# Opening stage: modulation on TensorE for three half parts of four, and another order of loads and stores

## The chip, the cores and the metric

The kernel runs on one core of a Trainium2 chip. The metric is the time of one execution in microseconds (us) on the device, of which the median of several runs is given. All data are float32 for 256 positions of width 1024.

## The reference

Two transformer blocks follow each other. The change touches the head of the first one alone:

```python
c_act = jax.nn.silu(c)
mod = c_act @ ada_w[l] + ada_b[l]
shift1, scale1, gate1, shift2, scale2, gate2 = [m[:, None, :] for m in jnp.split(mod, 6, axis=-1)]
h = rms_norm(x, norm1_g[l]) * (1 + scale1) + shift1
z = h @ w_in[l]
q, k, v, p, g_attn, g_pool = jnp.split(z, split_at, axis=-1)
```

`c` is one row of 1024 numbers and `ada_w` is 1024 x 6144, so `mod` is a product of one row with a matrix. Attention, pooling, the gates, a gated feed-forward block, and then a second block with a dense part and one with eight experts come behind. At the end of each of the second block's two layers stands `gate * (p[i] @ ple_proj_w[i])`; its product `p[i] @ ple_proj_w[i]` depends on inputs only, and the kernel computes it in the opening stage and parks it in memory.

## The kernel before, in words

Everything is held with features on the 128 partitions: `h` is a tile of 128 x 8 x 256 (feature in its group, group of features, position). A weight matrix is loaded in tiles of 128 x 4096 float32 (2 MB) named raw, of which there are three buffers used in turn (`load`, L138). To multiply nearly exactly at the speed of a narrow type, `split` (L158) makes of a piece of raw a high part (ScalarE copies it to a rounded type, L172, tile whi) and a low part (VectorE subtracts, L173, tile wlo), and `mm3` (L201) issues three products: high by high, high by low, low by high. Matmuls of other helpers go through `mm` (L199). A matmul of two plain float32 operands shows in the trace as two instructions.

The opening stage is written out by hand: within `tc.manual_schedule` (L623) VectorE, TensorE and ScalarE execute in the order in which the lines issue. SyncE issues the loads in the order in which they are written, and a load whose raw buffer is still read waits, with all that stand behind it on SyncE. The pieces are these:

- `Projected` (L557), once for each of two layers (e0 and e1): `parts` splits the two inputs, `sums(j)` makes 12 products of 256 columns for j from 0 to 3, so 48 in all, and `out(j)` copies the result from the accumulator; every second copy is stored to memory (tile kept, L586), issued by ScalarE.
- `rstd` (L265): the norm of `h`, summed over partitions by a matmul with a matrix of ones (L271), which is a part of the constants' tile ct, loaded at L366.
- `half_modulation` (L507), four times: part 1 is the scale and part 0 the shift, each in halves of 512 columns. A raw tile of `ada_w` is loaded in four pieces of 512 KB. `steps` lets VectorE multiply eight rows of 128 x 512 by `c` and add them up (L518, L520, into the tile sums); `total` sums that over the partitions with 8 matmuls by a column of ones; `put` adds `ada_b`.
- `scaled` (L533) and `shifted` (L538) put scale and shift of one half on `h` (tiles xn, and the pair xh and xl).
- `unit` (L544) splits a quarter of a half of `w_in`, and `products` (L548) multiplies it: 24 products of 256 columns, four units to each half, 96 a half. The first half of `w_in` comes in a raw tile, the second in a tile of its own (last_in).
- `distances` (L596) and `flipped` (L606): the bias of the attention, eight instructions of 512 columns on TensorE for four flips.

The order of TensorE before is: e0's sums, the norm's matmul and the distances among them; scale[0]'s sum ahead of e0's last sums; the e1 sums with shift[0]'s among them; the four products of the first half, with scale[1]'s sum after two of them; the four flips; shift[1]'s sum; the four products of the second half. In the code, `scale[0][0]`, `[1]` and `[2]` are steps, total and put:

```python
            scale[1][0](range(8))
            products(0, 1, us[1])
            scale[1][1]()
            products(0, 2, us[2])
            scale[1][2]()
            scaled(1)
            shift[1][0](range(8))
            products(0, 3, us[3])
```

Behind the manual order stand the norms of q and k, the value block of `w_in` (`gemm_v`), the attention, and the rest of the modulation: `modulation` (L384), stepped by VectorE along the following splits, which takes its loads of `ada_w` through the same raw buffers.

Of the kernel before, what the change touches and what calls it, by code (L numbers as in the profile page):

```python
# [10 lines left out]
F32 = mybir.dt.float32  # L11
# [4 lines left out]
OP = mybir.AluOpType  # L16
# [4 lines left out]
D = 1024  # L21
# [83 lines left out]
def kernel(ctx: ExitStack, tc: tile.TileContext, d, vat, cat, out, upto=99):  # L105
# [28 lines left out]

    raws = [wp, wp, wp]
    turn = [0]

    def load(src, pieces=1, columns=1, also=None):  # L138
# [6 lines left out]
        for i in range(0, a, a // pieces):  # L145
            for j in range(0, b, b // columns):
                ks, cs = slice(i, i + a // pieces), slice(j, j + b // columns)
                nc.sync.dma_start(v[:, ks, cs], src[:, ks, cs])
        if also is not None:
# [114 lines left out]

    def rstd(sq, n, both=False):  # L265

        o = bank("mm")[:, 0]
        if len(sq.parts) == 1:
            acc = sq.parts[0]
            dve.tensor_add(acc[:, 0], acc[:, 0], acc[:, 1])  # L270
            pe.matmul(o, cst("ones"), acc[:, 0], start=True, stop=True)  # L271
        else:
            for i in range(4):
                mm(o, cst("ones"), sq.parts[i // 2][:, i % 2], i == 0, i == 3)
        r = inv_sqrt(o, n, 256)
        return (r, o) if both else r
# [88 lines left out]
    nc.sync.dma_start(h, d["xT"])  # L365
    nc.sync.dma_start(ct, d["cst"])  # L366

# [127 lines left out]
    with stage("b1", po=1, acc=3, mm=4) as bp:  # L495
# [4 lines left out]
        xn = bp.tile([128, 8, 256], F32, name="xn", tag="ga")  # L500
        last_in = bp.tile([128, 4, 1024], F32, name="raw", tag="qkvp")


        sums = bp.tile([128, 4, 512], F32, name="sums", tag="gp")
        ps = [[bank("mm") for _ in range(2)] for _ in range(2)]

        def half_modulation(part, hf):  # L507

            at = part * 1024 + hf * 512
            o = part * 8 + hf * 4  # L510
            r = load(ada_w[:, :, at:at + 512], pieces=4)
            st = {}

            def steps(ks):
                for k in ks:
                    a, c = sums[:, 2 * (1 - part) + k % 2], sc[:, k:k + 1]
                    if k < 2:
                        dve.tensor_scalar(a, r[:, k], c, None, op0=OP.mult)  # L518
                    else:
                        dve.scalar_tensor_tensor(a, r[:, k], c, a, op0=OP.mult, op1=OP.add)  # L520

            def total():
                p = st["p"] = flat(bank("acc"))
                for i in range(2):
                    for j in range(4):
                        mm(p[:, j:j + 1], sums[:, 2 * (1 - part) + i, j * 128:j * 128 + 128],
                           cst("ones")[:, 0:1], i == 0 and j == 0, i == 1)

            def put():
                dve.tensor_add(mod[:, o:o + 4], st["p"][:, :4], vec[:, vat["ada_b"] + o:vat["ada_b"] + o + 4])  # L530
            return steps, total, put

# [24 lines left out]
        class Projected:  # L557
# [23 lines left out]
            def out(self):  # L581
# [3 lines left out]
                if j % 2:  # L585
                    nc.scalar.dma_start(kept[self.l][:, 2 * j - 2:2 * j + 2], t)  # L586

# [22 lines left out]

        scale, shift, ws = [], [], []
        scale.append(half_modulation(1, 0))
        second_projection = projection(1)
        shift.append(half_modulation(0, 0))
        ws.append(load(w_in[:, :4, :1024], pieces=2))
        scale.append(half_modulation(1, 1))
        shift.append(half_modulation(0, 1))
        for i in range(0, 4, 2):
            nc.sync.dma_start(last_in[:, i:i + 2], w_in[:, 4 + i:6 + i, :1024])
        ws.append(last_in)  # L620
        e0 = Projected(0, *first_projection, ("ath", "atl"))
        e1 = Projected(1, *second_projection, ("pqh", "pql"))
        with tc.manual_schedule(engines={dve.engine, pe.engine, act.engine}):  # L623
# [6 lines left out]
            e0.out()  # L630
            dve.tensor_copy(r1, rstd(sq, D))
            e0.out()
            e0.sums(2)
            distances()
            e0.out()
            scale[0][0](range(8))
            e0.sums(3)
            scale[0][1]()
            e0.out()
            e1.parts()  # L640
            scale[0][2]()
            scaled(0)
            e1.sums(0)
            e1.out()
            shift[0][0](range(8))
            e1.sums(1)
            e1.out()
            shift[0][1]()
            e1.sums(2)
            shift[0][2]()  # L650
            shifted(0)
            e1.out()
            e1.sums(3)
            us = [unit(0, 0)]
            e1.out()
            us += [unit(0, i) for i in range(1, 4)]
            products(0, 0, us[0])
            scale[1][0](range(8))
            products(0, 1, us[1])
            scale[1][1]()  # L660
            products(0, 2, us[2])
            scale[1][2]()
            scaled(1)
            shift[1][0](range(8))
            products(0, 3, us[3])
            for i in range(4):
                flipped(i)
            shift[1][1]()
            us = [unit(1, 0)]
            shift[1][2]()  # L670
            shifted(1)
            us += [unit(1, i) for i in range(1, 4)]
# [797 lines left out]
```

## Time and profile before

| | |
|---|---|
| median of 3 runs | 2002.33 us (2001.86 to 2008.63) |
| the profiled execution, its own time | 2010.97 us |
| its span, first to last instruction | 2009.2 us |
| mean granted TensorE clock in it | 0.984 |
| TensorE busy | 97% of the span |
| VectorE, ScalarE, GpSimd busy | 80%, 65%, 3% |
| read from memory | 531.19 MB |

A granted clock of 1.00 is the full clock and 0.50 half of it. Matmuls overlap in the pipeline, so the distance between two starts, not the duration of one, tells what a product costs; a merged line gives the time from the first start to the last end. An idle time is put down to what ended it. Times in the rows are counted from the span's start. The opening stage reaches to about 83 us.

### The profile page before, as it was taken

The numbers are of one execution on the slowest core, as the hardware profiler recorded it, in microseconds if no ns is written. First come the engines' busy times: TensorE is split into PE (matmuls) and PEld (weight loads), VectorE is DVE, ScalarE is ACT, GpSimd is POOL, SyncE is SP. The second block draws the span as 40 slices with busy tenths as digits, with TensorE's granted clock in tenths as the row PEclk, the third lists the DMA queues.
The fourth block names the chain that finished last, engine by engine and source line by source line (L and its number), as shares of the span: only waits on it lengthen the run. The fifth ranks groups of instructions, "written<-read, shape, count | busy, mean of one in ns | idle before, by whom it ended". The sixth has DMA issues, their size and how long they took to land. (4 is left out here: it accounts for less than half of the span.)

```text
span 2009.2 us, 29483 instructions
## 1 busy us (share of the span) xinstructions
PE 1950.1 (97%) x11943; PEld 1727.2 (86%) x11943; DVE 1598.9 (80%) x1898; ACT 1305.8 (65%) x1628; POOL 64.2 (3%) x64
## 2 busy tenths in 40 slices
PE   6999999999989999999999999999989999999998
PEld 5889899998989999989788888888868888888887
DVE  6667687777765555867799998889879888988988
ACT  4456465566554444665688787777767777777775
POOL 1002000000000000101200000000000000000000
PEclk8899999999999999999999999999999999999999
DMA  9566655463426454624599998999969999999990
GB/s 371 207 242 220 246 220 205 163 229 133 153 103 227 148 207 177 225 85 168 199 370 371 344 381 298 361 371 356 365 250 377 359 351 372 343 363 374 352 370 24
DMA packets 221681, 536.32 MB, mean 267 GB/s; under 512 B 4798, under 2 KB 8006, under 8 KB 221153
## 3 DMA queue, kind: packets, MB, share of 16 engines
q1 hardware_dynamic: 220560, 531.12, 72.4%
q8 instruction: 95, 1.56, 0.3%
q10 hardware_dynamic: 576, 2.10, 0.3%
q0 software_dynamic: 400, 1.15, 0.2%
q14 instruction: 50, 0.40, 0.1%
HBM read 531.19 MB, written 3.16 MB: 266 GB/s over the span
## 5 line engine op out<-in xcount | busy, mean ns | idle before, releaser
L173 DVE TENSOR_TENSOR wlo<-raw,whi 128x1024 fp32r<-128x1024 f32 (+1 forms) x949 | 1121.6, 1223 | 195.2 <-ACT whi L172 187.6
L172 ACT ACTIVATE whi<-raw 128x1024 fp32r<-128x1024 f32 (+1 forms) x957 | 983.0, 1055 | 380.6 <-PE pt L199 276.0
L199 PE MATMUL pt<-xh,whi 128*128 128x256 f32 x1536 | 444.5, 290 | 15.2 <-ACT xh L803 3.4
L199 PE MATMUL pt<-xl,whi 128*128 128x256 f32 x1536 | 442.5, 288 | 1.2 <-DVE xl L287 1.0
L199 PE MATMUL pt<-xh,wlo 128*128 128x256 f32 x1536 | 441.7, 288 | 1.8 <-DVE wlo L173 1.7
L199 PE MATMUL pt<-wlo,xh 128*128 128x512 f32 (+1 forms) x1000 | 381.4, 381 | 1.6 <-DVE wlo L173 1.6
L199 PE MATMUL pt<-whi,xl 128*128 128x512 f32 (+1 forms) x1000 | 381.9, 382 | 0.0
L199 PE MATMUL pt<-whi,xh 128*128 128x512 f32 (+1 forms) x1000 | 380.6, 381 | 0.2
L199 PEld LDWEIGHTS pt<-xh,whi 128*128 128x128 f32 x1536 | 299.8, 195 | 19.8 <-ACT xh L286 5.8
L199 PEld LDWEIGHTS pt<-xl,whi 128*128 128x128 f32 x1536 | 300.2, 195 | 5.2 <-issue 2.9
L199 PEld LDWEIGHTS pt<-xh,wlo 128*128 128x128 f32 x1536 | 300.3, 195 | 4.4 <-DVE wlo L173 2.4
L199 PEld LDWEIGHTS pt<-wlo,xh 128*128 128x128 f32 x1000 | 188.4, 188 | 40.7 <-DVE wlo L173 3.2
L199 PEld LDWEIGHTS pt<-whi,xh 128*128 128x128 f32 x1000 | 188.6, 189 | 36.2 <-ACT xh L1116 0.6
L199 PEld LDWEIGHTS pt<-whi,xl 128*128 128x128 f32 x1000 | 188.6, 189 | 34.8 <-issue 0.7
L199 PE MATMUL pt<-whi,gtl 128*128 128x512 f32 x448 | 178.9, 399 | 0.0
L199 PE MATMUL pt<-wlo,gth 128*128 128x512 f32 x448 | 177.3, 396 | 0.0
L199 PE MATMUL pt<-whi,gth 128*128 128x512 f32 x448 | 161.2, 403 | 0.0
L199 PE MATMUL fa<-gl,whi 128*128 128x256 f32 x400 | 112.6, 282 | 0.0
L199 PE MATMUL fa<-gh,whi 128*128 128x256 f32 x400 | 112.6, 281 | 0.0
L199 PE MATMUL fa<-gh,wlo 128*128 128x256 f32 x400 | 112.6, 281 | 0.0
L199 PEld LDWEIGHTS pt<-wlo,gth 128*128 128x128 f32 x448 | 84.2, 188 | 25.1 <-DVE wlo L173 4.6
L199 PEld LDWEIGHTS pt<-whi,gtl 128*128 128x128 f32 x448 | 84.3, 188 | 17.1
(296 smaller groups left out, 1995.9 us busy)
## 6 DMA issues: line engine op xcount, KB each, us to landing
raw<-in_moe_w_dram SPq DMA_DIRECT2D x168, 2048.0 KB, 9.1
raw<-in_dense_w_dram SPq DMA_DIRECT2D x21, 2048.0 KB, 7.9
raw<-in_w_in_dram SPq DMA_DIRECT2D x18, 2048.0 KB, 9.1
raw<-in_w_up_dram SPq DMA_DIRECT2D x10, 2048.0 KB, 10.1
raw<-in_ada_w_dram SPq DMA_DIRECT2D x16, 1024.0 KB, 7.8
raw<-in_w_down_dram SPq DMA_DIRECT2D x5, 2048.0 KB, 8.2
raw<-in_ada_w_dram SPq DMA_DIRECT2D x16, 512.0 KB, 11.4
raw<-in_w_o_dram SPq DMA_DIRECT2D x4, 2048.0 KB, 7.8
```

Of the source, the lines that this page charges most:

```text
L172: act.activation(hv, v, AF.Copy)
L173: eng.tensor_sub(lv, v, hv.bitcast(F32))
L199: pe.matmul(o, a, b, start=start, stop=stop, skip_group_check=True)
```

## The change

`half_modulation` becomes a class with the same parts. Three half parts are no longer stepped by VectorE: `total` multiplies the raw tile of `ada_w` (stationary) with the column of `c` (moving, one column) in 8 x 4 matmuls. The scale's second half is stepped by VectorE as before, from a tile of its own (fourth), and summed with a new tile of ones (ones1), which the norm's matmul takes as well and which GpSimd fills. The sums keep two tiles instead of four.

The loads come in another order: shift[0]'s half stands directly behind scale[0]'s, the second layer's projection behind them, the constants behind the scale's second half, and the second half of `w_in` now goes into a raw tile. The four stores of the projections are issued by SyncE, behind the last load of the opening, instead of ScalarE.

On TensorE, all of e0 comes first, with the distances ahead of the norm; then the long sums of scale[0] and shift[0] one behind the other; then e1; the four products of the first half without a break; the short sum of scale[1] and the long one of shift[1]; the flips; and the products of the second half.

```diff
--- before.py
+++ after.py
@@ -133,6 +133,7 @@
         return w.rearrange("(k p) n -> p k n", p=128)
 
     raws = [wp, wp, wp]
+    loaded = []
     turn = [0]
 
     def load(src, pieces=1, columns=1, also=None):
@@ -145,7 +146,7 @@
         for i in range(0, a, a // pieces):
             for j in range(0, b, b // columns):
                 ks, cs = slice(i, i + a // pieces), slice(j, j + b // columns)
-                nc.sync.dma_start(v[:, ks, cs], src[:, ks, cs])
+                loaded[:] = [nc.sync.dma_start(v[:, ks, cs], src[:, ks, cs]).ins]
         if also is not None:
             _, c, e = also.shape
             w = t[:, a * b:a * b + c * e].rearrange("p (a b) -> p a b", a=c)
@@ -262,13 +263,13 @@
         add.parts, add.n = st, 0
         return add
 
-    def rstd(sq, n, both=False):
+    def rstd(sq, n, both=False, ones=None):
 
         o = bank("mm")[:, 0]
         if len(sq.parts) == 1:
             acc = sq.parts[0]
             dve.tensor_add(acc[:, 0], acc[:, 0], acc[:, 1])
-            pe.matmul(o, cst("ones"), acc[:, 0], start=True, stop=True)
+            pe.matmul(o, cst("ones") if ones is None else ones, acc[:, 0], start=True, stop=True)
         else:
             for i in range(4):
                 mm(o, cst("ones"), sq.parts[i // 2][:, i % 2], i == 0, i == 3)
@@ -363,7 +364,6 @@
 
     first_projection = projection(0)
     nc.sync.dma_start(h, d["xT"])
-    nc.sync.dma_start(ct, d["cst"])
 
     sc = cp.tile([128, 8], F32, name="sc")
     c8 = vec[:, vat["c"]:vat["c"] + 8]
@@ -498,37 +498,44 @@
         w_in = rows(d["w_in"][0])
         x = pair([128, 8, 256], "x")
         xn = bp.tile([128, 8, 256], F32, name="xn", tag="ga")
-        last_in = bp.tile([128, 4, 1024], F32, name="raw", tag="qkvp")
-
-
-        sums = bp.tile([128, 4, 512], F32, name="sums", tag="gp")
+        fourth = bp.tile([128, 8, 512], F32, name="raw", tag="qkvp")
+        sums = bp.tile([128, 2, 512], F32, name="sums", tag="gp")
+        ones1 = bp.tile([128, 128], F32, name="ones1", tag="pdf")
+        nc.gpsimd.memset(ones1, 1.0)
+
+
         ps = [[bank("mm") for _ in range(2)] for _ in range(2)]
 
-        def half_modulation(part, hf):
-
-            at = part * 1024 + hf * 512
-            o = part * 8 + hf * 4
-            r = load(ada_w[:, :, at:at + 512], pieces=4)
-            st = {}
-
-            def steps(ks):
+        class HalfModulation:
+
+
+            def __init__(self, part, hf, r=None):
+                at = part * 1024 + hf * 512
+                self.o = part * 8 + hf * 4
+                src = ada_w[:, :, at:at + 512]
+                self.r = load(src, pieces=4) if r is None else r
+                if r is not None:
+                    for k in range(0, 8, 2):
+                        nc.sync.dma_start(r[:, k:k + 2], src[:, k:k + 2])
+
+            def steps(self, ks):
                 for k in ks:
-                    a, c = sums[:, 2 * (1 - part) + k % 2], sc[:, k:k + 1]
+                    a, c = sums[:, k % 2], sc[:, k:k + 1]
                     if k < 2:
-                        dve.tensor_scalar(a, r[:, k], c, None, op0=OP.mult)
+                        dve.tensor_scalar(a, self.r[:, k], c, None, op0=OP.mult)
                     else:
-                        dve.scalar_tensor_tensor(a, r[:, k], c, a, op0=OP.mult, op1=OP.add)
-
-            def total():
-                p = st["p"] = flat(bank("acc"))
-                for i in range(2):
+                        dve.scalar_tensor_tensor(a, self.r[:, k], c, a, op0=OP.mult, op1=OP.add)
+
+            def total(self, src=None, n=8):
+                self.p = flat(bank("acc"))
+                for k in range(n):
                     for j in range(4):
-                        mm(p[:, j:j + 1], sums[:, 2 * (1 - part) + i, j * 128:j * 128 + 128],
-                           cst("ones")[:, 0:1], i == 0 and j == 0, i == 1)
-
-            def put():
-                dve.tensor_add(mod[:, o:o + 4], st["p"][:, :4], vec[:, vat["ada_b"] + o:vat["ada_b"] + o + 4])
-            return steps, total, put
+                        mm(self.p[:, j:j + 1], (self.r if src is None else src)[:, k, j * 128:(j + 1) * 128],
+                           sc[:, k:k + 1] if src is None else ones1[:, 0:1], k == j == 0, k == n - 1)
+
+            def put(self):
+                o = self.o
+                dve.tensor_add(mod[:, o:o + 4], self.p[:, :4], vec[:, vat["ada_b"] + o:vat["ada_b"] + o + 4])
 
         def scaled(hf):
             gains("norm1_g", 0, 4 * hf, 4)
@@ -583,7 +590,8 @@
                 o = 2 * (j % 2)
                 act.activation(t[:, o:o + 2], p, AF.Copy)
                 if j % 2:
-                    nc.scalar.dma_start(kept[self.l][:, 2 * j - 2:2 * j + 2], t)
+                    with tc.issue_after(loaded[0]):
+                        nc.sync.dma_start(kept[self.l][:, 2 * j - 2:2 * j + 2], t)
 
         rb = bp.tile([BUCKETS + 1, H], F32, name="rb")
         oh = bp.tile([BUCKETS + 1, 384], F32, name="ohb", tag="wt", bufs=2)
@@ -609,15 +617,14 @@
             act.activation(bias[:, 2 * i:2 * i + 2], pf, AF.Copy)
 
         scale, shift, ws = [], [], []
-        scale.append(half_modulation(1, 0))
+        scale.append(HalfModulation(1, 0))
+        shift.append(HalfModulation(0, 0))
         second_projection = projection(1)
-        shift.append(half_modulation(0, 0))
         ws.append(load(w_in[:, :4, :1024], pieces=2))
-        scale.append(half_modulation(1, 1))
-        shift.append(half_modulation(0, 1))
-        for i in range(0, 4, 2):
-            nc.sync.dma_start(last_in[:, i:i + 2], w_in[:, 4 + i:6 + i, :1024])
-        ws.append(last_in)
+        scale.append(HalfModulation(1, 1, fourth))
+        nc.sync.dma_start(ct, d["cst"])
+        shift.append(HalfModulation(0, 1))
+        ws.append(load(w_in[:, 4:, :1024], pieces=2))
         e0 = Projected(0, *first_projection, ("ath", "atl"))
         e1 = Projected(1, *second_projection, ("pqh", "pql"))
         with tc.manual_schedule(engines={dve.engine, pe.engine, act.engine}):
@@ -628,47 +635,43 @@
                 sq(h[:, 2 * j:2 * j + 2])
             e0.sums(1)
             e0.out()
-            dve.tensor_copy(r1, rstd(sq, D))
-            e0.out()
-            e0.sums(2)
             distances()
             e0.out()
-            scale[0][0](range(8))
+            dve.tensor_copy(r1, rstd(sq, D, ones=ones1))
+            e0.sums(2)
+            e0.out()
             e0.sums(3)
-            scale[0][1]()
             e0.out()
+            scale[0].total()
+            scale[0].put()
+            scaled(0)
+            shift[0].total()
             e1.parts()
-            scale[0][2]()
-            scaled(0)
+            shift[0].put()
+            shifted(0)
             e1.sums(0)
             e1.out()
-            shift[0][0](range(8))
             e1.sums(1)
             e1.out()
-            shift[0][1]()
             e1.sums(2)
-            shift[0][2]()
-            shifted(0)
+            us = [unit(0, 0)]
             e1.out()
             e1.sums(3)
-            us = [unit(0, 0)]
+            us += [unit(0, 1)]
             e1.out()
-            us += [unit(0, i) for i in range(1, 4)]
-            products(0, 0, us[0])
-            scale[1][0](range(8))
-            products(0, 1, us[1])
-            scale[1][1]()
-            products(0, 2, us[2])
-            scale[1][2]()
+            us += [unit(0, i) for i in range(2, 4)]
+            scale[1].steps(range(8))
+            for i in range(4):
+                products(0, i, us[i])
+            scale[1].total(sums, 2)
+            scale[1].put()
             scaled(1)
-            shift[1][0](range(8))
-            products(0, 3, us[3])
+            shift[1].total()
+            shift[1].put()
+            us = [unit(1, 0)]
+            shifted(1)
             for i in range(4):
                 flipped(i)
-            shift[1][1]()
-            us = [unit(1, 0)]
-            shift[1][2]()
-            shifted(1)
             us += [unit(1, i) for i in range(1, 4)]
             for i in range(4):
                 products(1, i, us[i])
```

## Rows read from the trace of the kernel before

**Rows 1.** The page, part 1: TensorE's busy us, share, instructions.

```profile
PE 1950.1 (97%) x11943; PEld 1727.2 (86%) x11943; DVE 1598.9 (80%) x1898; ACT 1305.8 (65%) x1628; POOL 64.2 (3%) x64
```

**Rows 2.** Windows: length, busy PE, PEld, DVE, ACT, POOL, clock, DMA share, GB/s.

```profile
0.00:20.00 20.00, 10.18 (x52) 8.86 (x52) 9.53 (x23) 9.20 (x15) 4.34 (x10) 1.00 0.92 336
20.00:40.00 20.00, 14.79 (x74) 14.60 (x74) 15.16 (x28) 6.61 (x12) 0.95 (x1) 0.66 1.04 393
40.00:60.00 20.00, 16.32 (x99) 15.74 (x98) 14.87 (x25) 4.51 (x6) 0.00 (x0) 0.75 1.04 396
60.00:80.00 20.00, 18.04 (x116) 15.84 (x115) 12.83 (x17) 10.96 (x16) 0.00 (x0) 0.91 0.54 207
```

**Rows 3.** Timeline of TensorE: start, us, instructions, [idle before <-releaser].

```profile
23.16 3.54 PE L199 MATMUL pt<-ct,sums 128*128 128x1 f32 x16 [3.12 <-DVE sums L520]
...
33.06 3.55 PE L199 MATMUL pt<-ct,sums 128*128 128x1 f32 x16 [2.09 <-DVE sums L520]
...
50.97 3.54 PE L199 MATMUL pt<-ct,sums 128*128 128x1 f32 x16 [2.93 <-DVE sums L520]
...
62.77 3.60 PE L608 MATMUL pt<-bias,ct 128*128 128x512 f32 x8
66.20 1.84 PE L199 MATMUL pt<-ct,sums 128*128 128x1 f32 x16
69.87 0.38 PE L199 MATMUL pt<-xh,whi 128*128 128x256 f32 x1 [1.82 <-ACT xh L540]
...
121.88 1.84 PE L199 MATMUL pt<-ct,acc 128*128 128x1 f32 x16
```

**Rows 4.** DMA issues from 41.5 to 44.5 us: count, KB each, us to landing.

```profile
raw<-in_w_in_dram SPq DMA_DIRECT2D x2, 1024.0 KB, 12.5
```

**Rows 5.** The instructions on the tile sums, VectorE's part: ns least/median/most.

```profile
L520 DVE SCALAR_TENSOR_TENSOR sums<-raw,sc,sums x24: 742/744/748, 19.6 to 60.6; 128x512 f32<-128x512 f32 x24
L518 DVE TENSOR_SCALAR sums<-raw,sc x8: 477/479/483, 18.8 to 56.9; 128x512 f32<-128x512 f32 x8
```

**Rows 6.** Timeline of TensorE: single products of 256 columns.

```profile
41.01 0.39 PE L199 MATMUL pt<-xh,whi 128*128 128x256 f32 x1
...
47.64 0.28 PE L199 MATMUL pt<-xl,whi 128*128 128x256 f32 x1
47.76 0.28 PE L199 MATMUL pt<-xh,wlo 128*128 128x256 f32 x1
...
54.73 0.41 PE L199 MATMUL pt<-xl,whi 128*128 128x256 f32 x1
54.94 0.41 PE L199 MATMUL pt<-xh,wlo 128*128 128x256 f32 x1
```

**Rows 7.** Windows around the modulation's sums (columns as in group 2).

```profile
23.10:26.50 3.40, 3.33 (x16) 3.37 (x16) 3.40 (x4) 0.50 (x1) 0.95 (x1) 0.50 1.04 403
26.60:29.50 2.90, 2.90 (x15) 2.90 (x16) 2.69 (x8) 0.00 (x0) 0.00 (x0) 0.50 1.04 393
36.50:39.70 3.20, 3.20 (x16) 3.20 (x17) 1.84 (x5) 1.99 (x5) 0.00 (x0) 0.50 1.03 393
54.40:60.20 5.80, 5.80 (x28) 5.80 (x29) 5.58 (x13) 0.00 (x0) 0.00 (x0) 0.50 1.05 389
66.90:70.00 3.10, 1.27 (x12) 1.19 (x11) 1.45 (x3) 1.74 (x4) 0.00 (x0) 1.00 1.03 383
70.40:73.90 3.50, 3.50 (x16) 3.50 (x17) 3.50 (x6) 3.50 (x6) 0.00 (x0) 0.51 0.06 23
```

**Rows 8.** Windows around one sum of sixteen in a later stage.

```profile
121.90:125.10 3.20, 3.20 (x28) 2.92 (x26) 1.34 (x3) 0.57 (x2) 0.00 (x0) 0.99 0.02 7
125.10:128.40 3.30, 3.30 (x13) 2.21 (x11) 1.27 (x3) 0.49 (x1) 0.00 (x0) 0.50 0.48 102
```

**Rows 9.** Windows of two waits of TensorE for VectorE.

```profile
20.10:23.10 3.00, 0.00 (x0) 0.00 (x0) 3.00 (x6) 2.60 (x4) 0.00 (x0) 0.93 1.05 405
47.90:50.90 3.00, 0.14 (x2) 0.00 (x0) 3.00 (x6) 0.00 (x0) 0.00 (x0) 0.84 1.04 401
```

## The prediction

> **What bounds the kernel.** The page's totals say that TensorE is busy nearly throughout [rows 1], so time lost in the opening finds hardly any idle time later in which it could be won back, and whatever moves the opening moves the end. The edit lies in the first 83 us, so I read the windows of 20 us next [rows 2]: there TensorE is not full before 60 us (10.2, 14.8 and 16.3 of 20), the DMA engines are full from 20 to 60 us (share 1.04) and then half empty, and the granted clock is 0.66 and 0.75 in the middle two. Two things compete, then: loads and the chain of the modulation. The idle time ahead of TensorE decides between them. It waits for the VectorE sums three times (3.12, 2.09, 2.93 us), and for the shifted activations at 69.87 us [rows 3]; the last wait that the timeline shows ahead of the second four products is that one. The pieces of the last w_in load were issued by 43.1 us and need 12.5 us [rows 4], so they are there at about 56 us, 14 us before their products start. The chain is the bound at the end of the opening, not the loads.
>
> **Prices.** A half part of the modulation costs VectorE 2 x 0.479 + 6 x 0.744 = 5.4 us by mean durations; the starts overlap, and the stretches are 4.9 us [rows 5]. TensorE then sums in 16 instructions of one column for 8 matmuls, two each: 3.54 us at the low clock, 0.221 us each, and 1.84 us at the high one, 0.115 us each [rows 3]. A 256-column product follows the one before it by 0.12 us at the high clock (47.64 to 47.76) and 0.21 us at the low (54.73 to 54.94) [rows 6]. The bias flips are 8 instructions in 3.60 us, 0.45 us each, at the high clock [rows 3].
>
> **What is removed and added.** Three of the four halves lose their VectorE steps, some 15 us of VectorE, and their TensorE sums grow from 8 matmuls to 32, so from 16 instructions to 64: 64 x 0.115 = 7.3 us at the high clock, 64 x 0.221 = 14.2 us at the low one. These lie on TensorE, in its fixed order, with the e1 products or the flips queued behind them. Which clock they get is the whole question. A long run of such instructions is not in this trace; the nearest rows are the short ones. In 23.10 to 26.50 us TensorE is busy 3.33 us with sixteen of them alone and the clock is 0.50; it is 0.50 for the next 2.9 us too, while 256-column products run, and rises only behind these. From 36.50, after the second sixteen, it is the same for 3.2 us [rows 7]. In the stretch 121.90 to 125.10 us TensorE is busy 3.20 of 3.20 us, with sixteen of them (1.84 us from 121.88 [rows 3]) and other narrow work in it, and the clock, at 0.99 there, is 0.50 in the next 3.3 us [rows 8]. So they do not raise the clock, and a busy engine lost it around them. I take it that a run of 64 loses the high clock (1.00, which is 2.4 GHz) soon after its start and has the low one (1.2 GHz) to its end. Bounds: 7.3 and 14.2 us a half part.
>
> The Trainium skill ("TensorE: Matmul & The Clock Gate", "Why this matters for your kernels") has it that the clock falls back when TensorE idles between bursts, and asks that it be kept busy. By that rule 64 instructions without a gap would keep the high clock, and the time would be that of the first rival below. The trace does not agree: the busy stretch of [rows 8], 3.20 of 3.20 us, was followed by a grant of 0.50.
>
> **The sum**, along TensorE. How long the high clock outlasts the last wide product: it fell within the idle 20.1 to 23.1 and 47.9 to 50.9 us, with mean grants of 0.93 and 0.84 [rows 9], so 2.6 and 2.0 us into them (0.84 is 2.0 at 1.00 and 1.0 at 0.50); I take 2.6, from the same place. Behind the flips it outlasted 66.9 to 70.0 us too, some 4 us [rows 7]. How long wide products run at the low clock before it rises: 2.9, 3.2, 5.8 and 3.5 us [rows 7]; I take 4.
> 1. The e0 products end at about 20 us, as before (their loads come first in both orders; the constants' 592 KB behind them cost nothing there, since the ones for the norm are now made by a GpSimd memset). scale[0]: 2.6 us at the high clock do 22 of 64, the other 42 take 9.3 us: done at 31.9. shift[0]: 14.2 us: 46.1. The 48 e1 products: 4 us do 19, the other 29 take 3.5 us: 53.6. Before, the first four products began at 41.01 [rows 6]: 12.6 us later.
> 2. The first four products run without a break, 96 x 0.12 = 11.5 us: 65.1. scale[1], the half that VectorE keeps, has been stepped beside them, and its 16 instructions take 1.8 us: 66.9. Before, the flips began at 62.77 [rows 3] with this behind it: 4.1 us later. Here the change gives back two waits and a slow stretch.
> 3. shift[1]: 0.8 us of high clock are left and do 7; 57 take 12.6 us: 80.3. The flips, formerly ahead of these sums and at the high clock, come behind: at the low one I estimate 0.8 us each (0.45 x 0.21/0.12), five in 4 us, then three in 1.4: 85.7. The shift on ScalarE and VectorE takes 1.8 us (the idle time at 69.87 [rows 3]) and hides beside the flips. Before: 69.87.
> 4. The last four products: 11.5 us, now wholly at the high clock: 97.2. Before they had 3.5 to 4 us of low clock: 19 in 4 us, 77 in 9.2, so 83.1. That is 14.1 us later.
>
> **What costs nothing, and its cover.** The loads of w_in's first half wait for scale[0]'s buffer, now freed at 31.9 us; with the 12.5 us that such a load took under full queues [rows 4] they are there by 45, wanted at 53. Behind that wait, on SyncE's queue, stands every later load: ada_w's half for VectorE's steps comes some 5 us after, by 50, and VectorE is at it from about 57. ada_w's last half waits for shift[0] (46.1), there by 58, wanted at 67. w_in's second half goes behind it, there by 65, wanted at 85. The four stores of 512 KB leave ScalarE's queue and stand in SyncE's ahead of the value block's load: 2 MB, some 5 us at 390 GB/s [rows 2]; it is there at about 75 and wanted at 97. The next ada_w load waits for shift[1]'s buffer (80.3) and may be up to 6 us late for VectorE's first step at about 86; the last four products, 11.5 us, cover that. The constants land near 46 us; their first user on TensorE is the flip. If the covers go, 6 us is the largest of these.
>
> The profiled execution took 2010.97 us around its span of 2009.2, 0.4% above the median of the three runs, 2002.33 us; the 14.1 us are a difference within it, so I add them to the median: **2016.4 us**.
>
> **Rivals.**
> - *The high clock lasts through the one-column runs* (not slower). It decides in scale[0] and shift[0]: where the grant is still 1.00 after 30 us. Then each half costs 7.3 us: scale[0] ends at 27.3, shift[0] at 34.6, the e1 products (48 x 0.12 = 5.8) at 40.4, the first four at 51.9, scale[1] at 53.7, shift[1] at 61.0, flips 64.6, the last four 76.1: 7 us sooner than 83.1, 1995.3 us. For it: a run of sixteen from 66.20 us had the high clock to its end [rows 3]. Against it: [rows 7, 8]. Break-even is at 0.152 us an instruction: 192 of them gain 7 us at 0.115 and lose 13 at 0.221. Chance 0.13.
> - *The loads were the bound, and the order frees them* (faster): ada_w's two first halves come together, and the stores leave their way. The last four products would then start when w_in has landed, near 58 us instead of 69.87: 12 us sooner, 1990 us. For it: a DMA share of 1.04 to 60 us [rows 2]. Against: those pieces waited 14 us for their products. Chance 0.05.
> - *A load is late as well* (slower still): the 6 us above, or the first half of w_in, which the slow scale[0] delays: 2022 us. Chance 0.06.
> - *The clock falls in one or two of the three long sums only*, or holds for 4 us more in each: 2003 to 2011 us. Chance 0.10. That the change does not do what it says has no place here: the order of TensorE is written out by hand.
>
> **Numbers.** The forecast has 0.66. Its own range: with 4 us of high clock at each start [rows 7] and 2.9 us of low clock behind it, 5 us less; with no high clock in them and 5.8 us behind, 5 us more: 2011 to 2021.5. To leave out no more than 2 in 10 the range goes down to the first rival: 1995 to 2021.5. A measurement of this kernel can tell about 0.5%, 10 us, from no change: slower by more, 0.63 (nine tenths of the forecast, and the late load, less a little since the sum is only 4 us beyond that bound); within, 0.29; faster by more, 0.08 (the second rival, and a little of the first if it goes further).
>
> **What will show it.** The one-column rows of the new kernel: 64 a run, some 12 to 14 us long, with a grant of 0.50 behind their first 2 to 3 us; VectorE with a quarter of these steps; the last four products starting at 84 to 87 us. Wrong would be: runs of 7.3 us at 1.00; products waiting for a raw tile's DMA; VectorE waiting for a load of ada_w past 100 us.

## The result, and the profile after

The kernel after the change takes **2023.78 us** (median of 4 runs, 2018.95 to 2026.58), the kernel before 2002.42 us beside it (2001.86 to 2008.63): a ratio of **1.0083, interval 1.0063 to 1.0103**. It is slower, as forecast; the 2016.4 us forecast were 7.4 us too few, and the range ended 2.3 us below the measurement. As a ratio the forecast was 2016.4 / 2002.33 = 1.0070, within the interval. The quotient of the two medians, 1.0107, lies above the interval; it rests on four executions of the kernel before, three of them at the low end of its spread, so the size of the loss is known to a few tenths of a per cent only. Apart from one slow execution of 2139 us, the kernel before takes anywhere from 2001 to 2012 us. So ratios with their intervals are used from here on.

The page's totals of after stand beside [rows 1]:

```profile
PE 1969.9 (97%) x12087; PEld 1746.6 (86%) x12087; DVE 1584.0 (78%) x1874; ACT 1305.6 (65%) x1628; POOL 66.9 (3%) x65
```

TensorE has 144 instructions more (three sums of 64 for three of 16) and is busy 20 us longer; VectorE has 24 fewer and 15 us less. Windows of 20 us of after, columns as in [rows 2]:

```profile
20.00:40.00 20.00, 20.00 (x115) 20.00 (x115) 4.87 (x9) 2.59 (x4) 0.95 (x1) 0.61 0.91 333
40.00:60.00 20.00, 20.00 (x149) 20.00 (x149) 11.69 (x19) 8.74 (x13) 0.00 (x0) 0.87 0.97 358
60.00:80.00 20.00, 20.00 (x113) 17.25 (x112) 5.31 (x13) 5.50 (x10) 0.00 (x0) 0.74 0.56 205
```

Where TensorE waited before, it is now full from 20 to 80 us, and no wait for sums is left. Yet the clock granted there is no better (0.61, 0.87, 0.74 for 0.66, 0.75, 0.91). The timeline of after's TensorE says what fills it, columns as in [rows 3]:

```profile
19.27 22.48 PE L200 MATMUL pt<-sc,raw 128*128 128x1 f32 x128
...
60.50 1.84 PE L200 MATMUL pt<-ones,sums 128*128 128x1 f32 x16
...
62.20 10.78 PE L200 MATMUL pt<-sc,raw 128*128 128x1 f32 x64
72.84 5.12 PE L616 MATMUL pt<-bias,ct 128*128 128x512 f32 x8
77.40 0.68 PE L200 MATMUL pt<-xh,whi 128*128 128x256 f32 x1
```

The long sums of scale[0] and shift[0] are one run of 128 instructions of one column, 22.48 us; shift[1]'s takes 10.78 us. The last four products start at 77.40 us, 7.5 us later than before. Windows within and behind the long sums (columns as in [rows 2]):

```profile
19.30:24.50 5.20, 5.20 (x50) 5.20 (x48) 0.14 (x1) 0.60 (x1) 0.95 (x1) 1.00 1.03 376
24.60:41.60 17.00, 17.00 (x81) 17.00 (x82) 4.87 (x9) 2.52 (x3) 0.00 (x0) 0.50 0.89 330
41.70:45.00 3.30, 3.30 (x17) 3.30 (x17) 1.84 (x5) 2.14 (x5) 0.00 (x0) 0.50 0.67 188
...
62.20:65.40 3.20, 3.20 (x31) 3.20 (x30) 2.00 (x6) 0.00 (x0) 0.00 (x0) 1.00 0.92 341
65.60:72.80 7.20, 7.20 (x35) 7.20 (x36) 0.00 (x0) 0.00 (x0) 0.00 (x0) 0.50 0.03 12
```

Both long runs begin at a grant of 1.00 (2.4 GHz), lose it after 5.3 and 3.3 us, and stay at 0.50 (1.2 GHz) to their end, with TensorE busy 17.00 of 17.00 and 7.20 of 7.20 us. The wide products behind them start at 0.50 too.

The opening ends where ScalarE takes q from the accumulators. Two places mark the path from there: that copy, and the second norm's gain on VectorE (L420), the end of the attention's preparation. (TensorE's last products of the opening end 3.4 us behind the start of that copy, in before and in after; the expectations below name now the one, now the other.) The first fence is ScalarE's timeline of before, the second its VectorE, the third and fourth the same of after:

```profile
79.99 0.69 ACT L682 ACTIVATE qkvp<-pt,qg 128x512 f32<-128x512 f32 x1 [1.22 <-PE pt L199]
```

```profile
175.14 0.16 DVE L420 SCALAR_TENSOR_TENSOR gm<-mod,vec 128x8 f32<-128x8 f32 x1
```

```profile
85.95 0.69 ACT L685 ACTIVATE qkvp<-pt,qg 128x512 f32<-128x512 f32 x1 [4.51 <-PE pt L200]
```

```profile
186.90 0.16 DVE L420 SCALAR_TENSOR_TENSOR gm<-mod,vec 128x8 f32<-128x8 f32 x1
```

The copy is 6.0 us later and the gain 11.8 us; the span is 11.8 us longer as well (2021.0 for 2009.2). So in these two profiles nothing is won back or lost behind 187 us. Of the 11.8 us, half arise in the opening, and the other 5.8 in a stretch whose code the diff doesn't touch.

### The profile page after: what moved, and what is told of

Read it like the earlier page. It is cut to its first block, busy times and chain, and to the rows that moved or that the text cites. A ratio compares the mean times of both kernels' runs of the same rounds, so it can differ in the third digit from the quotient of the medians.

```text
span 2021.0 us, 29737 instructions
## 1 busy us (share of the span) xinstructions
PE 1969.9 (97%) x12087; PEld 1746.6 (86%) x12087; DVE 1584.0 (78%) x1874; ACT 1305.6 (65%) x1628; POOL 66.9 (3%) x65
## 5 line engine op out<-in xcount | busy, mean ns | idle before, releaser
L200 PE MATMUL pt<-xh,whi 128*128 128x256 f32 x1536 | 442.9, 289 | 13.3 <-ACT xh L806 3.4
```

Source lines behind the costliest of these rows:

```text
L200: pe.matmul(o, a, b, start=start, stop=stop, skip_group_check=True)
```

## The experiments

Each kernel is compared with the kernel before by its ratio and interval. The two marks of each profiled execution, in us, stand together here; the stretch is the second less the first:

| kernel | q copy starts | gain ends | stretch | span | ratio [interval] |
|---|---|---|---|---|---|
| before | 80.0 | 175.3 | 95.3 | 2009.2 | 1 |
| after | 86.0 | 187.1 | 101.1 | 2021.0 | 1.0083 [1.0063, 1.0103] |
| after, again | 93.1 | 191.7 | 98.6 | 2025.9 | 1.0094 [1.0076, 1.0112] |
| 128 columns | 71.8 | 166.8 | 95.0 | 1998.0 | 0.9968 [0.9953, 0.9982] |
| multiplication alone | 95.6 | 193.2 | 97.6 | 2024.7 | 1.0107 [1.0086, 1.0127] |
| order alone | 83.5 | 179.4 | 95.9 | 2014.6 | 1.0013 [0.9999, 1.0026] |
| stores on ScalarE | 89.9 | 183.8 | 93.9 | 2014.8 | 1.0051 [1.0033, 1.0068] |
| stores late | 92.7 | 196.8 | 104.1 | 2025.8 | 1.0087 [1.0061, 1.0112] |
| a sum twice | 100.8 | 199.3 | 98.5 | 2030.6 | 1.0178 [1.0155, 1.0200] |
| mixed | 64.0 | 161.8 | 97.8 | 1990.5 | 0.9948 [0.9930, 0.9967] |
| mixed, one column | 69.0 | 170.4 | 101.4 | 2004.1 | 0.9977 [0.9961, 0.9993] |
| mixed, ScalarE | 69.7 | 163.2 | 93.5 | 1997.1 | 0.9956 [0.9942, 0.9971] |

**128 columns.** My theory is that the clock is the loss; the rival, that the instructions themselves or the order are. The moving column is repeated over 128 columns, so that each sum comes out 128 times, of which one is kept:

```diff
-  mm(self.p[:, j:j + 1], (self.r if src is None else src)[:, k, j * 128:(j + 1) * 128],
-     sc[:, k:k + 1] if src is None else ones1[:, 0:1], k == j == 0, k == n - 1)
+  c = sc[:, k:k + 1].to_broadcast([128, 128]) if src is None else ones1
+  mm(self.p[:, j * 128:(j + 1) * 128], v[:, k, j * 128:(j + 1) * 128], c, k == j == 0, k == n - 1)
```

> The changed kernel with one edit: the moving operand of the modulation's sums is the column repeated 128 times (128 columns instead of 1), so each instruction does more and the same number is issued; put reads one column of each group. Theory (the long sums are slow since TensorE's clock falls during one-column work): the grant stays at 1.00 through the sums, 128 instructions take about 15.5 us instead of 22.5 and 64 about 7.8 instead of 10.7, the last opening products end some 12 us sooner, near 76 to 77 us, and the whole is faster than the changed kernel by about 1% and than the kernel before by 0.3 to 0.4% (0.996). Rival (TensorE is slow in these sums for the weight loads, whatever the moving width, or loses the clock with every short matmul): the sums stay at 0.21 us an instruction or become slower, and the ratio to before stays at 1.008 or above.

TensorE's timeline, then its windows, of this kernel:

```profile
19.54 14.46 PE L200 MATMUL pt<-sc,raw 128*128 128x128 f32 x128
...
52.91 7.31 PE L200 MATMUL pt<-sc,raw 128*128 128x128 f32 x64
```

```profile
19.50:34.00 14.50, 14.50 (x132) 14.50 (x131) 5.08 (x10) 3.12 (x4) 0.95 (x1) 1.00 0.95 342
52.90:60.00 7.10, 7.10 (x66) 7.10 (x65) 2.00 (x6) 0.00 (x0) 0.00 (x0) 1.00 1.03 392
```

The ratio is 0.9968, against 0.996 expected. The same 192 instructions on 128 times the columns take 21.8 us instead of 33.3, at a grant of 1.00 throughout: 14.46 / 128 = 0.113 us each. The clock is shown to be the loss in the opening, which ends 14.2 us sooner (71.8 for 86.0); the rival falls. The span is 23.0 us shorter (1998.0 for 2021.0), but 6.1 us of that arise in the stretch behind the opening, where ScalarE's order is another one too, and 2.7 us behind the stretch, so they are not shown to be the sums' clock.

**Multiplication alone, order alone.** The first takes the kernel before and lets TensorE multiply the three halves, the rest untouched. The second takes the kernel after and gives the three halves back to VectorE.

```diff
-            scale[0][0](range(8))
             e0.sums(3)
-            scale[0][1]()
+            scale[0][3]()      # 8 x 4 matmuls on the raw tile; likewise shift[0], shift[1]
```

> The kernel before with the multiplication alone: the same three halves are summed by TensorE from the raw tile in 64 one-column instructions each, while loads, stores and the order of everything else stay as they were. Theory (the cost lies in the one-column sums): each run takes 10.5 to 13.6 us in place of 4.9 us of VectorE and 3.5 of TensorE, the last opening products end near 100 us (96 to 102) instead of 83, and the ratio to before is 1.007 to 1.009. Rival (the cost of the change lies in its order of loads and stores): the ratio is within 0.2% of 1.

```diff
-            scale[0].total()
+            scale[0].steps(range(8))
+            scale[0].total(sums, 2)    # likewise shift[0], shift[1]
```

> The changed kernel with VectorE's steps put back for the three halves, at the places of its long sums: its order of loads, stores and products alone. Theory (the order costs little, the sums cost): the last opening products end near 86.5 us (85.5 to 87.5), 3 us later than before, and the ratio to before is 1.000 to 1.003. Rival (the order of loads and stores costs): 1.006 or more.

TensorE's timeline of the multiplication alone, and then of the order alone:

```profile
19.63 8.79 PE L199 MATMUL pt<-sc,raw 128*128 128x1 f32 x64
...
32.77 11.43 PE L199 MATMUL pt<-sc,raw 128*128 128x1 f32 x64
...
73.30 11.03 PE L199 MATMUL pt<-sc,raw 128*128 128x1 f32 x64
```

```profile
24.48 3.54 PE L200 MATMUL pt<-ones,sums 128*128 128x1 f32 x16 [4.26 <-DVE sums L527]
...
34.38 3.54 PE L200 MATMUL pt<-ones,sums 128*128 128x1 f32 x16 [6.36 <-DVE sums L527]
...
65.91 3.54 PE L200 MATMUL pt<-ones,sums 128*128 128x1 f32 x16 [6.35 <-DVE sums L527]
```

The multiplication alone came out at 1.0107, a little above what I expected: at least as slow as the whole change, so the new order does not cause the loss. The order alone, 1.0013, cannot be told from no change, though TensorE waits 17.0 us for sums in it, more than the 8.1 us of [rows 3]. Either waits of TensorE or narrow instructions at 0.50 fill this opening; the change trades the one for the other and pays more.

**The same kernel again, and a sum twice.** The program of after, unchanged, profiled anew; and shift[1]'s long sum issued twice, the first result kept, which prices one such sum.

> The changed kernel itself, once more, beside the others. Both theories: the ratio to before lies within the interval of the first comparison, 1.006 to 1.010; its opening ends between 86 and 93 us, by how long the clock holds in its long sums.

```diff
             shift[1].total()
+            kept_p = shift[1].p
+            shift[1].total()
+            shift[1].p = kept_p
             shift[1].put()
```

> The changed kernel with the long sum of the shift's second half computed twice, the second result thrown away: 64 more one-column instructions in a place where the clock has fallen. Theory (they run at the low clock and nothing covers them): the run grows from 10.7 to about 24.3 us, 13.6 more at 0.213 us each, and the ratio to before goes to about 1.014. Rival (the high clock comes back, or the work is covered): 7.3 us more, or none: 1.012 or 1.008.

TensorE's timeline of the unchanged program's second profile, and that of the doubled sum:

```profile
19.94 25.03 PE L200 MATMUL pt<-sc,raw 128*128 128x1 f32 x128
...
64.38 1.84 PE L200 MATMUL pt<-ones,sums 128*128 128x1 f32 x16
...
66.08 13.13 PE L200 MATMUL pt<-sc,raw 128*128 128x1 f32 x64
79.07 6.06 PE L616 MATMUL pt<-bias,ct 128*128 128x512 f32 x8
```

```profile
61.72 24.59 PE L200 MATMUL pt<-sc,raw 128*128 128x1 f32 x128
86.18 6.66 PE L616 MATMUL pt<-bias,ct 128*128 128x512 f32 x8
```

One program has an opening that ends at 86.0 us in one execution and at 93.1 in another: each long run kept the grant of 1.00 for less time in the second (25.03 for 22.48 us, 13.13 for 10.78), and the flips behind it are slower. The doubled sum takes 13.8 us more than the single one in after's first profile, 0.216 us an instruction, as a wholly low clock would have it, and the ratio, 1.0178, is 0.8 to 0.95% above after's, more than the 1.014 I expected. Its profile is of the fastest of four executions (2032.37 us, the others 2040.5 to 2041); where the others lost 8 us is not shown.

**Stores on ScalarE, stores late.** These ask for the 5.8 us behind the opening. The first issues the four stores from ScalarE again. The second leaves them on SyncE but behind the value block's load; my explanation then was that the stores delay this load in the planned order, so that its splits stand behind the norm of q. (Behind the manual order each engine's order is planned when the program is built, and it need not be that of the lines: in after and in the first of these two the same lines stand in another order on ScalarE.)

```diff
-                    with tc.issue_after(loaded[0]):
-                        nc.sync.dma_start(kept[self.l][:, 2 * j - 2:2 * j + 2], t)
+                    nc.scalar.dma_start(kept[self.l][:, 2 * j - 2:2 * j + 2], t)
```

> The changed kernel with its four stores of the projections issued by ScalarE again, as before. Behind the opening the changed kernel lost another 5.5 us in its profile: the first split of the value block stands behind the norm of q in ScalarE's order, and with the stores moved back it stands ahead again, six splits in a row. Theory (that order is the second part of the loss): the opening ends as in the changed kernel (89 to 96 us), no gap of TensorE follows the norm of q, and the ratio to before falls from 1.008 to 1.004 or 1.006. Rival (the order there is covered, the loss comes from the opening's end alone): 1.008 remains. A third: the stores in the way of the loads cost more than they give, and it is above 1.008.

```diff
-        gemm_v(block(w_in, 2), x,
+        value = block(w_in, 2)
+        for o, t in pending:     # the four stores, put off
+            with tc.issue_after(loaded[0]):
+                nc.sync.dma_start(o, t)
+        gemm_v(value, x,
```

> The changed kernel with its four stores still on SyncE, but behind the value block's load instead of ahead of it. Theory (the stores' place changes the order in which ScalarE splits the value block, and that order costs): six splits stand in a row again ahead of the q copies, no gap of TensorE follows the norm of q, and the ratio to before is that of the variant with the stores on ScalarE, 1.004 to 1.006. Rival (the queue that issues the stores, or the time that their transfers take from the loads, is what counts): as the changed kernel, 1.007 to 1.009.

First ScalarE's timeline of after, at the gap in question; then the windows behind the opening, of after and of the stores on ScalarE:

```profile
91.23 0.27 ACT L197 ACTIVATE ry<-pt,eps 128x16 f32<-128x16 f32 x1 [3.04 <-PE pt L200]
91.40 1.05 ACT L173 ACTIVATE whi<-raw 128x1024 fp32r<-128x1024 f32 x1
```

```profile
85.00:95.00 10.00, 7.82 (x61) 7.53 (x60) 2.52 (x5) 6.01 (x11) 0.00 (x0) 0.89 0.51 193
95.00:105.00 10.00, 10.00 (x57) 8.49 (x57) 8.41 (x13) 4.94 (x8) 0.00 (x0) 0.77 0.06 10
```

```profile
85.00:95.00 10.00, 10.00 (x87) 10.00 (x86) 8.47 (x8) 6.49 (x9) 0.00 (x0) 1.00 0.59 212
95.00:105.00 10.00, 10.00 (x73) 8.93 (x74) 8.18 (x13) 6.56 (x12) 0.00 (x0) 1.00 0.69 238
```

In after, ScalarE waits 3.04 us for the norm of q with the value block's split behind it, and TensorE has a gap and a clock of 0.89 and 0.77. TensorE's timeline of after has the gap as two waits for the halves of that split:

```profile
92.50 0.39 PE L200 MATMUL pt<-whi,xh 128*128 128x256 f32 x1 [1.31 <-ACT whi L173]
93.76 0.58 PE L200 MATMUL pt<-wlo,xh 128*128 128x256 f32 x1 [0.87 <-DVE wlo L174]
```

The same two waits stand in the second profile of after and in that of the doubled sum, and in no profile of another kernel. The whole stretch as a window, first of after, then of after again (columns as in [rows 2]):

```profile
85.95:187.06 101.11, 96.02 (x671) 84.21 (x670) 71.49 (x114) 64.12 (x127) 17.59 (x28) 0.95 0.59 211
```

```profile
93.12:191.66 98.54, 93.26 (x671) 82.34 (x670) 71.13 (x114) 64.02 (x127) 17.61 (x28) 0.98 0.61 217
```

TensorE is idle for 5.1 and 5.3 us of it, where before has 2.2 us; the clock is 0.95 in the first and 0.98 in the second, as in before. Taking what the clock costs as the length times what is missing to 1.00, an estimate from these windows, the 5.8 us that the first profile loses here are 2.9 us of waits and some 3 us of clock, and the 3.3 us of the second are nearly all waits (3.0). With the stores on ScalarE TensorE is full at 1.00 and the stretch is 93.9 us for 101.1. The ratio, 1.0051, is what was expected; its interval lies below that of after's second comparison (1.0076 to 1.0112), though not below that of the first. But with the stores late on SyncE the stretch is not shorter; it is 104.1 us, and the ratio 1.0087. TensorE's timeline of that kernel shows other waits, and its window a low clock:

```profile
114.68 0.58 PE L200 MATMUL pt<-xh,wlo 128*128 128x256 f32 x1 [2.06 <-DVE wlo L174]
...
141.38 0.39 PE L200 MATMUL pt<-xh,whi 128*128 128x256 f32 x1 [2.50 <-ACT whi L173]
```

```profile
115.00:125.00 10.00, 10.00 (x50) 7.85 (x49) 6.98 (x11) 4.46 (x12) 0.00 (x0) 0.69 0.00 0
```

So my explanation falls as I put it: the late stores do set the split ahead of the norm of q again, and the two waits behind it are gone, but others come in their place (6.8 us of idle TensorE in the stretch, at a clock of 0.93). What is shown is that the place of four stores alone moves this stretch, by up to 10 us between single executions (after's own two differ by 2.5), and that it moves through TensorE's waits for splits and the clock around them. What makes the order come out one way or the other is not shown: the 128 columns and the order alone have the stores on SyncE as after has, the split ahead of the norm, and stretches of 95.0 and 95.9, so the stores do not cost it in every case.

**Mixed.** If the clock and the waits are both costs, each half should go where neither arises: scale[0] by TensorE on 128 columns, the other three on VectorE beside TensorE's other work, the flips two ahead of and two behind shift[1]'s sum, and the stores late.

```diff
             scale[0].total()
+            shift[0].steps(range(8))
+            e1.parts()
             scale[0].put()
             scaled(0)
-            shift[0].total()
-            e1.parts()
+            shift[0].total(shift[0].sums, 2)
...
-            scale[1].total(sums, 2)
+            scale[1].total(scale[1].sums, 2)
+            shift[1].steps(range(8))
```

> A version meant to beat both: the changed kernel's loads; the scale's first half summed by TensorE with 128 moving columns; the three others stepped by VectorE beside TensorE's work, the shift's first half while the scale's runs and the second while the first products run; the 16 instructions of their sums with 128 columns too; the flips two before and two behind the last sum; the stores on SyncE behind the value block's load. Theory (TensorE's own chain bounds the opening, and the clock holds as long as the work is wide): the grant is 1.00 from about 15 us on, the q copies start at 64 to 67 us instead of 71.8 in the wide variant and 80 before, and the ratio to before is 0.993 to 0.995. Rival (the loads bound it by then, w_in's second half landing near 52 us, or VectorE does): the q copies start at 70 or later, 0.996 or more.

TensorE's timeline of it, and windows:

```profile
19.05 7.31 PE L200 MATMUL pt<-sc,raw 128*128 128x128 f32 x64
26.20 1.95 PE L200 MATMUL pt<-ones,sums 128*128 128x128 f32 x16
```

```profile
20.00:40.00 20.00, 18.15 (x156) 17.95 (x156) 15.53 (x26) 10.07 (x15) 0.95 (x1) 1.00 1.02 370
40.00:60.00 20.00, 19.26 (x138) 16.60 (x138) 16.96 (x33) 8.16 (x13) 0.00 (x0) 1.00 1.04 399
60.00:80.00 20.00, 20.00 (x159) 18.93 (x158) 15.16 (x21) 12.74 (x20) 0.00 (x0) 1.00 0.93 350
```

Its ratio is the lowest of all, 0.9948 at 1993.26 us (1992.31 to 1997.41), within what was expected, and it beats both kernels. The opening ends at 64.0 us. TensorE is nearly full at 1.00 and, unlike in after, the DMA engines are full too (1.02, 1.04).

Two kernels take one part out of it: one column instead of 128, and the stores issued by ScalarE.

> The mixed version with one moving column in its sums instead of 128, all else the same. Theory (one-column work loses the clock): the run of 64 takes about 9 us instead of 7.3 and is at 0.50 at its end, the e1 products behind it start at the low clock, and the q copies start at 67 to 72 us instead of 64; ratio to before 0.996 to 0.999. Rival (the mixed version's gain is that of VectorE's steps beside TensorE alone): as the mixed version, 0.995.

> The mixed version with the stores issued by ScalarE, as before, instead of SyncE behind the value block's load. Theory (where the stores are issued sets the order behind the opening, and ScalarE's place gave the shortest stretch from the q copies to the end of the first block's attention stage, 93.9 us by the gains of the second norm, against 97.8 in the mixed version): the opening ends within 2 us of 64, the stretch is 93 to 95.5 us, ratio 0.992 to 0.994. Rival (that stretch varies for other reasons): 0.995 or more.

TensorE's timeline with one column and a window of that kernel, then a window with the stores on ScalarE:

```profile
19.94 9.13 PE L200 MATMUL pt<-sc,raw 128*128 128x1 f32 x64
28.94 3.55 PE L200 MATMUL pt<-ones,sums 128*128 128x1 f32 x16
...
52.41 1.84 PE L200 MATMUL pt<-ones,sums 128*128 128x1 f32 x16
```

```profile
45.00:60.00 15.00, 14.96 (x105) 12.42 (x103) 13.29 (x29) 3.12 (x6) 0.00 (x0) 1.00 1.04 396
```

```profile
55.00:65.00 10.00, 7.90 (x50) 6.09 (x50) 7.93 (x17) 6.86 (x11) 0.00 (x0) 1.00 1.03 396
```

One column gives 0.9977, as expected: 5.0 us are lost in the opening and the stretch is 3.6 us longer. The stores on ScalarE missed: the stretch is short (93.5 us) as in the other kernel with them there, but the opening ends at 69.7 us, where I expected 64. At a DMA share of 1.03 TensorE is busy only 7.90 of 10 us, and from 20 to 40 us ScalarE waits 8.4 us for the load of e1's input, in the mixed kernel 4.7: this opening is near the bound of the loads. That the 2 MB of stores among them are what delays it is not shown; that load is issued 3.1 us later than in the mixed kernel (16.3 for 13.3 us), ahead of the first store at 17.0. Its interval overlaps that of mixed.

## Why the prediction was right, and where it was off

**The choice of the clock was right.** "A run of 64 loses the high clock soon after its start and has the low one to its end" is what the windows of after show, and the 128 columns show that it is the cause. The Trainium skill ("TensorE: Matmul & The Clock Gate", "Why this matters for your kernels") counts idle time between bursts as what loses the clock; here TensorE was busy 17.00 of 17.00 us at 0.50, so in this case idle time is not all that loses it, and the measurement decides. The first rival fell with it, but its price was well worked out: 0.115 us an instruction became 0.113 in the kernel that kept the clock, which took 1999.65 us at 0.9968, where the rival had 1995.3, 0.9965 of the median.

**Step 1** had the run of 128 end at 46.1 us; it ended at 41.8 and, in the second profile, at 45.0. Two terms were mis-sized. The high clock lasted 5.3 us and not 2.6 in the first profile. And an instruction at the low clock costs 0.213 us, not 0.221 (the distance of the starts in after from 26 to 41 us; the doubled sum gives 0.216): I divided 3.54 us by 16, which counts the whole duration of the last instruction, where the distance of starts is the price.

**Steps 2 and 3**: the short sum ended at 62.3 us (66.2 in the second profile) for 66.9; shift[1]'s took 10.8 (13.1) for 13.4; the flips 5.1 (6.1) for 5.4.

**Step 4**: the last four products started at 77.4 us (84.6 in the second profile) for 85.7, and the opening cost 6.0 us in one execution and 13.1 in the other, for 14.1. The sum took the short end of a quantity that varies between executions: how long the grant outlasts the last wide product. I had given it 2.6 us with 4 us as the far bound, from waits of TensorE and not from busy runs; it reached 5.3 in the first profile, and 3.3 us of shift[1]'s sum had the high clock where I had 0.8. In the second profile both came out as forecast (2.5 and 0.7 us), and the opening there cost nearly what the sum says.

**The step that failed is "what costs nothing, and its cover".** I priced the stores' move at nothing, since the value block's load would be there at 75 us and wanted at 97, and bounded a failed cover by 6 us without putting it into the forecast. The stretch behind the opening grew by 5.8 and 3.3 us in the two profiles, and 6.4 to 8.6 us (0.32 to 0.43%) came back with the stores on ScalarE. It was no late load: from 80 to 195 us the waits of after's first profile name none, and those of the second name one of 0.8 us. The value block's load was issued at 53.1 us and there 15.7 us later, at 69, sooner than I had it. What the waits name more of is VectorE waiting for ScalarE's half of a split; the first fence is the waits of before in that stretch, the second those of after (us in total, times, longest):

```profile
DVE wlo L173 <- ACT whi L172: 9.1, 8, 2.7
```

```profile
DVE wlo L174 <- ACT whi L173: 20.1, 9, 9.4
```

In the second profile they are 18.2 us, with the stores on ScalarE 10.3. The order of the work there is what changed, and TensorE's waits with it, 2.9 and 3.0 us more than before; why the order changed is not shown. The error of step 4 and this one go against each other: the spans differ by 11.8 and 16.7 us, for 14.1. That the sum came out so near in the first profile is luck in this respect. The miss in absolute time lies in the base. Against the profiled execution, as the sum was made, it gives 2010.97 + 14.1 = 2025.1 us, and 2022.76 was measured; I then added it to the median, which came from the faster of the executions shown.

**Nothing won back later** was right: from 187 us on the difference stays at 11.8 us. The second rival (loads as the bound) fell for this kernel, since no product waited for a raw tile; it comes nearest in the mixed kernels, once the chain is short, where ScalarE's splits wait for a load.

## What to carry to other kernels

Price an instruction moved to TensorE at the clock that its own run will have, and look in the trace for what followed the nearest such run, however busy the engine was. A matmul of one column may cost as much as one of 128 at the same clock, so try the wide form before the move is given up. And when a DMA's issue moves past a stage that is ordered by hand, price the stage behind it as well, where a planner lays out the order.

## What had not been expected of the hardware

- More columns made it faster: 128 instructions with one moving column took 22.48 and 25.03 us, with 128 columns 14.46 us.
- One program's opening differed by 7.1 us between two executions (86.0 and 93.1 us), most of it in the long narrow runs (2.6 and 2.4 us) and the work right behind them.
- A short narrow run need not lose the clock. In the mixed kernel with one column the run of 64 lost it (0.59 from 24 to 29 us), but the grant stayed at 1.00 from 45 to 60 us around a sum of sixteen with one column at 52.41 us and another at 55.92 us. With 128 columns the grant was 1.00 from 20 to 80 us (mixed). Such a sum shows 1.84 to 1.94 us with one column and 1.95 us with 128, all at the high clock.
